# An encoder trunk on one core: where six weight pieces are split a second time

## The chip, the cores and the metric

The kernel runs on one core of a Trainium2 chip. The metric is the device time of one execution in microseconds (us). The engines are PE (TensorE, matrix products), DVE (VectorE), ACT (ScalarE), POOL (GpSimd) and SP (SyncE, which only issues transfers here). SBUF is the memory on the core, PSUM the accumulator memory in banks of 512 float32 per partition, DRAM the memory outside. Each engine works through its own instructions in order and waits for the others by semaphores.

## The reference

A two-layer encoder over a sequence of 2048 tokens (x_prompt) and one of 512 (x_sample), width 1024, all in float32.

```python
h = rmsnorm(x, g);  z = h @ w_in                      # 1024 -> 1024 (q) + 256 (k) + 256 (v) + 1024 (gate)
o = banded_gqa_with_sink(q, k, v, rel_bias, sink)     # 16 heads of 64, 4 k/v heads, |i-j| <= 128
x = x + (o * silu(gate)) @ w_out                      # layer 0
h = rmsnorm(x, g);  f = fftn(h, positions and 256 channels of each group).real
x = x + (f * silu(h @ w_gate)) @ w_out                # layer 1
y = rmsnorm(x, gf)
```

Both sequences go through the same weights. What the change touches is layer 0's projection weight w_in, 1024 x 2560.

## The kernel before

**Split products.** The products keep nearly float32 accuracy by splitting each operand in two parts of the type fp32r: a high part, which is a cast of the value, and a low part, which is the value less the high part. `matmul3` (lines 91 to 95) adds three products: high by high, high by low, low by high. So each weight piece must be split before use: one cast on ACT (line 107) and one subtract on DVE (line 114) or in four pieces on POOL (line 112).

**Weight pieces.** w_in is cut into 20 pieces of 128 x 1024 (512 KB): 0 to 7 are q for the eight head pairs, 8 and 9 are k, 10 and 11 are v, 12 to 19 the gate for the eight head pairs. Pieces 20 to 27 are w_out. A split piece has 1 MB (both parts) and lies in a tile `w`, of which there are four buffers (tag "w"). `load_w` (line 97) gives a piece to the caller.

**Chunks.** Layer 0 runs in five chunks of 512 tokens (`CHUNKS`): chunk 0 is the sequence of 512 tokens, chunks 1 to 4 are the long one. Chunk 0 loads the raw pieces from w_in and w_out, splits them and, for most, stores both parts in DRAM (`wsd`). Chunks 1 to 4 load the split parts from `wsd` in one transfer of 1 MB (line 101). The first six pieces that chunk 0 uses (8, 9, 10, 11, 0, 12; `LATE`, line 34) are needed at once at the start; they are split with DVE (`lo_engine`) and not stored then. Later in chunk 0, at one place in each of the head pairs 1 to 6 (lines 655 and 656), one of the six is loaded from w_in once more, into another `w` buffer, split with ACT and POOL, and stored to `wsd`. These are the tiles `w32late` and `wlate`; nothing in chunk 0 reads them.

**The order within a chunk.** `make_h` (line 166) loads x transposed in eight slices (`xk`), multiplies with the norm factor on POOL (line 180) and splits the slices into h, on ACT and DVE (lines 184 and 185); for a chunk that has a neighbour to its right there are 128 halo columns more (`hl`, lines 190 and 191). `kv_proj` (line 244) makes k (`kp`, two banks; 48 matmuls), the halo's k (`kh`), and v (`vp`, four tokens blocks in four banks, then one for the halo). k is copied to `kwin` by ACT and DVE in turn (lines 261 and 262), `kh` by ACT (line 283). Then the q and gate products of head pair 0 follow, and a loop over 64 steps (eight head pairs, four blocks of 128 tokens, two heads), with scores (line 396), exponential (line 412, ACT), transposes (line 432), their split (lines 433 and 434) and the product with v (line 446). Between these stand the q and gate products of the next head pair (`qp`, `gp`), and the tanh of the gate (line 351). During the last head pairs `stats` (line 135) makes the sums of squares for the next chunk (tiles `xs`), and `spread` (line 149) turns them into a row for the norm: DVE writes a diagonal `dg` (line 158), PE multiplies it with ones (`ib`, line 162).

**The seam between two chunks.** The output projection has two halves of four banks (`op`). The first half runs among the last steps of the loop. The second half, the `tail`, runs at the seam, followed by `kv_proj` of the next chunk. `evac` (line 508) adds the residual x to each of the four banks on DVE (line 516) in tiles `xr`, of which there are three buffers, and SP stores them to `x1d` (line 517). So the fourth residual tile of a half is loaded only when the first one of that half has been stored. There are six banks: k and v of the next chunk use those that the tail's evacuations free.

**Buffers that bear on the change.** The raw pieces, the slices `xk` and the tiles `xs` share four buffers of 4 KB per partition (`xtile`, tag "x"). Who comes later in the program waits until the one that had the buffer before is done. A scheduler places the instructions of each engine by its own estimate of their times within what data and buffers allow; lines 123 and 124 let the kernel add an order of issue.

Of the kernel before, what the change touches and what calls it, by code (L numbers as in the profile page):

```python
# [8 lines left out]
F32 = mybir.dt.float32  # L9
# [4 lines left out]
ALU = mybir.AluOpType  # L14
# [4 lines left out]
P = 128  # L19
D = 1024  # L20
# [10 lines left out]
BIG = 1.0e30  # L31
LINE = 512
HALVES = ((1, 0), (1, 1), (0, 0), (0, 1))
LATE = (0, 8, 9, 10, 11, 12)
CH = 512
CHUNKS = [(2048, SEQ, T), (0, 0, SEQ), (512, 0, SEQ), (1024, 0, SEQ), (1536, 0, SEQ)]

# [1 line left out]
def f32(ap):  # L39
    return ap.bitcast(F32)  # L40
# [3 lines left out]
def encoder(  # L44
# [3 lines left out]
    PE, ACT, DVE, POOL, SP = nc.tensor, nc.scalar, nc.vector, nc.gpsimd, nc.sync  # L48
# [22 lines left out]
    wsd = [dram.tile([P, 2, D], F32R, name=f"wsd{i}") for i in range(28)]  # L71
# [7 lines left out]
    def xtile(shape, dtype, name):  # L79
        return xp.tile(shape, dtype, align_bytes=LINE, tag="x", bufs=4, name=name)  # L80
# [13 lines left out]
        PE.matmul(out, a[0], b[1], start=False, stop=False, skip_group_check=more)  # L94
        PE.matmul(out, a[1], b[0], start=False, stop=stop, skip_group_check=more)  # L95

    def load_w(c, n, name, lo_engine=None, late=None):

        w = wp.tile([P, 2, D], F32R, align_bytes=LINE, tag="w", bufs=4, name=f"w{name}")
        if c:  # L100
            SP.dma_start(f32(w), f32(wsd[n]))
            return w[:, 0], w[:, 1]
        w32 = stage[late is not None or n > 19 or n in (6, 7, 18, 19)](f"w32{name}")
        load = SP.dma_start(w32, w_in[n] if n < 20 else w_out[(n - 20) // 4, (n - 20) % 4])
        if late:
            after(load, late)
        ACT.copy(w[:, 0], w32)  # L107
        if lo_engine is None:

            for i in range(4):  # L110
                cs = slice(i * 256, i * 256 + 256)
                POOL.tensor_tensor(w[:, 1, cs], w32[:, cs], f32(w[:, 0, cs]), ALU.subtract)
        else:
            lo_engine.tensor_tensor(w[:, 1], w32, f32(w[:, 0]), ALU.subtract)
        if late or n not in LATE:
            (SP if lo_engine else POOL).dma_start(f32(wsd[n]), f32(w))
        return w[:, 0], w[:, 1]

    stage, res_tile, ready = [], [], {}

    def after(ins, anchor):

        if anchor is not None:
            tc.add_manual_dep(ins.ins, anchor.ins.name, ISSUE, reason="issue order")

    def attention_phase():

        with ExitStack() as es:
# [6 lines left out]
            def stats(c):  # L135

                tok, lo_t, hi_t = CHUNKS[c]
                nt = min(640, hi_t - tok) // P
                ss = main.tile([P, 8], F32, tag="ss", bufs=2, name=f"ss{c}")

                def one(i):
                    xt = xtile([P, D], F32, f"xs{c}_{i}")
                    after(SP.dma_start(xt, x[tok + i * P : tok + (i + 1) * P, :]), last_exp[0])
                    sq = ACT.activation(xt, xt, AF.Square, accum_out=ss[:, i : i + 1])
                    after(sq, last_exp[0])

                return [lambda i=i: one(i) for i in range(nt)] + [lambda: inv_rms(ss, nt, f"inv{c}")]

            def spread(c, inv):

                tok, lo_t, hi_t = CHUNKS[c]
                nt = min(640, hi_t - tok) // P
                invb = ap.tile([P, 640], F32, tag="invb", name=f"invb{c}")
                for i0 in range(0, nt, 4):
                    m = min(4, nt - i0)
                    ps = bank(f"ib{c}_{i0}")
                    dg = ap.tile([P, 4, P], F32, tag="tmp", bufs=2, name=f"dg{c}_{i0}")
                    DVE.tensor_tensor(
                        dg[:, :m], ident.unsqueeze(1).to_broadcast([P, m, P]),
                        inv[:, i0 : i0 + m].unsqueeze(2).to_broadcast([P, m, P]), ALU.mult,  # L160
                    )
                    PE.matmul(ps[:, : m * P], ones, dg[:, :m].rearrange("p i q -> p (i q)"), start=True, stop=True)
                    ACT.copy(invb[:, i0 * P : (i0 + m) * P], ps[:, : m * P])
                return invb
# [36 lines left out]
            for i in range(WARM):  # L201
                PE.matmul(ps, idle[:, :P], idle, start=True, stop=True)

            early = [load_w(0, 8, "k0_0", DVE)]
            hs, halo = make_h(0, None)
            early.append(load_w(0, 9, "k0_1", DVE))

            def bias_rows():
# [27 lines left out]
            last_exp, last_evac, last_mul = [None], [None], [None]  # L236
# [7 lines left out]
            def kv_proj(c, hs, halo, norms=None, early=None):  # L244
# [9 lines left out]
                def evac_k(t, ps, n, wc):  # L254
                    ps = scaled(ps, invb, f"k{t}")
                    for j in range(2):
# [3 lines left out]
                        for rows in (slice(0, 64), slice(64, 128)):  # L260
                            ACT.copy(kw[rows, 0, cs], sp)
                            DVE.tensor_tensor(kw[rows, 1, cs], sp, f32(kw[rows, 0, cs]), ALU.subtract)

                wk = early or [load_w(c, 8 + t, f"k{c}_{t}", DVE) for t in range(2)]

                def wslice(w, k, c0, n):
# [341 lines left out]
            for c in range(len(CHUNKS)):  # L608

                if c > 1:  # L610
                    hs, halo = make_h(c, invb)
                for s in tail:
                    s()
                if c == 1:
                    hs, halo = make_h(c, invb)
                if c:
                    invb0 = kv_proj(c, hs, halo)
                else:
                    invb0 = kv_proj(c, hs, halo, first_norms, early)
                rowd, sk = bias  # L620
                uTs = []
                res = [{} for p in range(8)]
                at = [attention(c, p, res[p], uTs) for p in range(8)]
                for s in qg_proj(c, 0, hs, res[0], invb0):
                    s()
                at[0][0]()
                fill = []
                for i in range(64 + LAG + AVLAG):
                    p, n = divmod(i, 8)
                    if n == 0 and i < 64:  # L630
                        if p < 7:

                            fill = qg_proj(c, p + 1, hs, res[p + 1], invb0)
                            fill.pop(0)()
                            at[p + 1][0]()
                            if i == 0 and c == 0:

                                for s in fill[:8]:
                                    s()
                                fill = fill[8:]  # L640
                        else:
                            op = out_proj(c, uTs)
                            fill, rest, tail = op[:4], op[4:7], op[7:]
                    if c + 1 < len(CHUNKS):
                        if i == 24:
                            norm_steps = stats(c + 1)
                        if i >= 28 and i % 4 == 0 and norm_steps:
                            inv = norm_steps.pop(0)()
                        elif i == 56:
                            invb = spread(c + 1, inv)  # L650
                    if i in (4, 8, 12, 16) and c in EXTRA:
                        EXTRA[c].pop(0)()
                    if c == len(CHUNKS) - 1 and i in AHEAD:
                        AHEAD[i]()
                    if c == 0 and i % 8 == 3 and 1 <= p < 7:
                        load_w(0, LATE[p - 1], f"late{p}", late=last_exp[0])
                    if i < 64:
                        at[p][1](*HB[n])
                    k = i - LAG
                    if 0 <= k < 64:  # L660
                        at[k // 8][2](*HB[k % 8])
                    if i < 64:
                        m = len(fill) * (n + 1) // 8 - len(fill) * n // 8
                        todo = fill[len(fill) * n // 8 :][:m]
                        for s in todo[: m // 2]:
                            s()
                    k -= AVLAG
                    if 0 <= k < 64 and k % 2 == 1:
                        b = k % 8 // 2
                        at[k // 8][3](b)  # L670
                        if b % 2 == 1:
                            at[k // 8][4](b)
                    if i < 64:
                        for s in todo[m // 2 :]:
                            s()
                    elif rest:
                        rest.pop(0)()
            return tail

    def fourier_phase(tail):  # L680
        with ExitStack() as es:
# [522 lines left out]
            for i, f in enumerate(pend):  # L1204
                finish(*f, last=i == len(pend) - 1)

    fourier_phase(attention_phase())


# [96 lines left out]
```

## Time and profile before

| | us |
|---|---|
| three runs, median | 1679.39 |
| lowest and highest | 1677.16, 1682.95 |
| the profiled execution, time | 1680.38 |
| the profiled execution, span | 1678.6 |
| PE busy | 1648.0 (98% of the span) |
| DVE busy | 1182.3 (70%) |
| ACT busy | 874.6 (52%) |
| POOL busy | 392.1 (23%) |
| moved by DMA | 344.69 MB, 205 GB/s |

Times in the profile are counted from the span's start. Chunk 0 reaches to about 240 us, where the k products of chunk 1 begin. A line of a timeline has the start, the duration, the engine, the line of the kernel, the operation, the tile that is written and those that are read, and in brackets the idle time of the engine before it and what ended it. A line of the waits has the waiting engine and line, what it waited for, the sum, the count and the longest.

### The profile page before, as it was taken

Reading aid. Unit: us, or ns where it says so; the run is one execution under the profiler, and the core shown is the slowest. Engines: PE = TensorE matmul, PEld = TensorE weight load, DVE = VectorE, ACT = ScalarE, POOL = GpSimd, SP = SyncE. Lnnn points to the kernel's source line nnn. Section 1 sums busy time; section 2 is a strip of 40 time slices with the busy share of each in tenths; the row PEclk is TensorE's granted clock in tenths of the full one; section 3 lists DMA queues with packets and bytes.
Section 4 is the critical chain, followed back from the end, with each engine's and each line's share of the span. In section 5 each row is a group of like instructions: output and inputs, shape, how many; then the busy total and the mean of one; then the engine's idle time right before and its main releaser. Section 6 shows DMA issues by size and latency. Waiting matters only on the chain.

```text
span 1678.6 us, 25638 instructions
## 1 busy us (share of the span) xinstructions
PE 1648.0 (98%) x8980; PEld 1413.9 (84%) x8980; DVE 1182.3 (70%) x2782; ACT 874.6 (52%) x1998; POOL 392.1 (23%) x544
## 2 busy tenths in 40 slices
PE   9999899999999999999999999999999999999998
PEld 6887778888898888988888888888888887888886
DVE  5788645888638886478874588758676768888553
ACT  6788624676326674256752466646554455343321
POOL 2466740211403122221114211121112121111000
PEclk9999999999999999999999999999999999999999
DMA  8487775454765455763548644556556468453331
GB/s 306 154 330 308 262 285 207 167 197 161 261 226 186 174 185 180 272 223 132 183 151 318 250 151 164 212 199 221 190 205 236 171 229 338 158 194 126 122 126 51
DMA packets 91341, 344.69 MB, mean 205 GB/s; under 512 B 11163, under 2 KB 21403, under 8 KB 73292
## 3 DMA queue, kind: packets, MB, share of 16 engines
q1 hardware_dynamic: 73404, 267.79, 45.6%
q0 software_dynamic: 17520, 74.46, 11.3%
q8 instruction: 72, 1.18, 0.3%
q10 hardware_dynamic: 288, 0.79, 0.2%
q14 instruction: 57, 0.47, 0.1%
HBM read 267.47 MB, written 75.53 MB: 204 GB/s over the span
## 4 chain that ended last, share of the span: by engine, by line
PE 85%; DVE 5%; ACT 4%; DMA 3%; issue 2%; POOL 1%; SPq 0%; DVEq 0%; POOLq 0%; ACTq 0%
PE av L446 6%; PE spt L396 6%; PE pt L432 6%; PE qp L93 4%; PE qp L95 4%; PE qp L94 4%; PE gp L93 4%; PE gp L95 4%; PE gp L94 4%; PE op L93 4%; PE fo L94 4%; PE fo L95 3%; PE op L95 3%; PE op L94 3%; PE fo L93 3%; PE W L93 2%
## 5 line engine op out<-in xcount | busy, mean ns | idle before, releaser
L412 ACT ACTIVATE S<-S 128x385 f32<-128x385 f32 (+1 forms) x320 | 191.1, 597 | 40.5 <-DVE S L408 39.7
L433 ACT CAST pts<-pt 128x384 fp32r<-128x384 f32 (+1 forms) x320 | 144.6, 455 | 118.9 <-PE pt L432 114.5
L434 DVE TENSOR_TENSOR pts<-pt,pts 128x384 fp32r<-128x384 f32 (+1 forms) x320 | 168.6, 527 | 47.6 <-ACT pts L433 44.3
L408 DVE CUSTOM_DVE_ANT_0 S<-spt,b 128x385 f32<-128x385 f32 (+1 forms) x320 | 168.9, 528 | 37.0 <-PE spt L396 32.1
L396 PE MATMUL spt<-kwin,qab 128*128 128x384 f32 (+1 forms) x640 | 158.7, 329 | 1.6 <-DVE S L408 1.6
L461 POOL TENSOR_TENSOR o<-o,s 128x256 f32<-128x256 f32 x75 | 55.4, 738 | 429.5 <-DVE o L457 423.3
L432 PE MATMUL pt<-ident,S 128*128 128x128 f32 x896 | 150.5, 274 | 0.0
L396 PEld LDWEIGHTS spt<-kwin,qab 128*128 128x128 f32 x640 | 119.0, 188 | 29.4 <-DVE S L408 2.7
L446 PEld LDWEIGHTS av<-pts,v 128*128 128x128 f32 x896 | 126.7, 189 | 16.0 <-DVE pts L434 3.1
L446 PE MATMUL av<-pts,v 128*128 128x256 f32 x896 | 136.6, 285 | 2.9 <-DVE pts L434 2.0
L93 PE MATMUL qp<-h,wq 128*128 128x512 f32 x320 | 137.2, 429 | 0.7 <-ACT wq L107 0.7
L93 PE MATMUL gp<-h,wg 128*128 128x512 f32 x320 | 137.8, 431 | 0.0
L418 DVE TENSOR_SCALAR S<-S 128x384 f32<-128x384 f32 (+1 forms) x288 | 129.9, 451 | 8.5
L93 PE MATMUL op<-wo,uT 128*128 128x512 f32 x320 | 127.0, 398 | 2.9 <-ACT uT L463 2.9
L93 PE MATMUL fo<-wo,tTu 128*128 128x512 f32 x320 | 125.8, 393 | 1.3 <-ACT wo L1108 1.3
L432 PEld LDWEIGHTS pt<-ident,S 128*128 128x128 f32 x896 | 114.2, 140 | 14.7 <-DVE pts L434 3.4
L95 PE MATMUL qp<-h,wq 128*128 128x512 f32 x320 | 126.2, 394 | 0.1
L94 PE MATMUL op<-wo,uT 128*128 128x512 f32 x320 | 125.9, 394 | 0.0
L95 PE MATMUL gp<-h,wg 128*128 128x512 f32 x320 | 125.8, 393 | 0.0
L94 PE MATMUL qp<-h,wq 128*128 128x512 f32 x320 | 125.8, 393 | 0.0
L94 PE MATMUL gp<-h,wg 128*128 128x512 f32 x320 | 125.7, 393 | 0.0
L94 PE MATMUL fo<-wo,tTu 128*128 128x512 f32 x320 | 125.4, 392 | 0.1
(341 smaller groups left out, 4113.8 us busy)
## 6 DMA issues: line engine op xcount, KB each, us to landing
wq<-wsd SPq DMA_DIRECT2D x32, 1024.0 KB, 4.8
wg<-wsd SPq DMA_DIRECT2D x32, 1024.0 KB, 5.6
wo<-wsd SPq DMA_DIRECT2D x32, 1024.0 KB, 4.9
x<-x1d SPq DMA_DIRECT2D x40, 512.0 KB, 3.7
b<-b21d SPq DMA_DIRECT2D x40, 512.0 KB, 5.9
b<-rowd SPq DMA_DIRECT2D x40, 384.0 KB, 4.2
xs<-in_x_dram SPq DMA_DIRECT2D x23, 512.0 KB, 6.6
s2d<-gt POOLq DMA_DIRECT2D x40, 256.0 KB, 4.1
```

Source lines behind the costliest of these rows:

```text
L93: PE.matmul(out, a[0], b[0], start=start, stop=False, skip_group_check=more)
L94: PE.matmul(out, a[0], b[1], start=False, stop=False, skip_group_check=more)
L95: PE.matmul(out, a[1], b[0], start=False, stop=stop, skip_group_check=more)
L396: PE.matmul(ps[:, 2 + k0 * P : 2 + k1 * P], q, kwin[g][:, part, b * P + k0 * P : b * P + k1 * P], start=part == 0, stop=part == 1,)
L408: DVE.tensor_tensor_reduce(out=s[:, e0:e1], in0=ps[:, 1 + e0 : 1 + e1], in1=st["bias"][:, j, 386 - e1 : 386 - e0][:, ::-1], scale=1.0, sca ...
L412: last_exp[0] = ACT.activation(s[:, e0:e1], s[:, e0:e1], AF.Exp, bias=mn, scale=-1.0, accum_out=den)
L418: DVE.tensor_scalar(s[:, ks], s[:, ks], den, None, ALU.mult)
L432: PE.transpose(ps[:, kb, :], s[:, 1 + kb * P : 1 + (kb + 1) * P], ident)
L433: ACT.copy(hi[:, k0:k1, j, :], ps[:, k0:k1, :])
L434: DVE.tensor_tensor(lo[:, k0:k1, j, :], ps[:, k0:k1, :], f32(hi[:, k0:k1, j, :]), ALU.subtract)
L446: PE.matmul(out, v, pt[:, kb].rearrange("p h q -> p (h q)"), start=kb == k0 and part == 0, stop=kb == k1 - 1 and part == 1,)
L461: eng.tensor_tensor(of, of, res["s"][:, cs], ALU.mult)
```

## The change

The six pieces are no longer loaded and split a second time within chunk 0. Instead chunk 1 loads them raw where it needs them, splits them with ACT and DVE, uses them, and stores the parts to `wsd` from POOL's queue for chunks 2 to 4. The list keeps its members and has another name. The raw tiles take x buffers.

```diff
-LATE = (0, 8, 9, 10, 11, 12)
+AGAIN = (0, 8, 9, 10, 11, 12)
...
-    def load_w(c, n, name, lo_engine=None, late=None):
+    def load_w(c, n, name, lo_engine=None):
 
         w = wp.tile([P, 2, D], F32R, align_bytes=LINE, tag="w", bufs=4, name=f"w{name}")
+        if c == 1 and n in AGAIN:
+            w32 = xtile([P, D], F32, f"w32{name}")
+            SP.dma_start(w32, w_in[n])
+            ACT.copy(w[:, 0], w32)
+            DVE.tensor_tensor(w[:, 1], w32, f32(w[:, 0]), ALU.subtract)
+            POOL.dma_start(f32(wsd[n]), f32(w))
+            return w[:, 0], w[:, 1]
         if c:
             SP.dma_start(f32(w), f32(wsd[n]))
             return w[:, 0], w[:, 1]
-        w32 = stage[late is not None or n > 19 or n in (6, 7, 18, 19)](f"w32{name}")
-        load = SP.dma_start(w32, w_in[n] if n < 20 else w_out[(n - 20) // 4, (n - 20) % 4])
-        if late:
-            after(load, late)
+        w32 = stage[n > 19 or n in (6, 7, 18, 19)](f"w32{name}")
+        SP.dma_start(w32, w_in[n] if n < 20 else w_out[(n - 20) // 4, (n - 20) % 4])
         ACT.copy(w[:, 0], w32)
...
-        if late or n not in LATE:
+        if n not in AGAIN:
             (SP if lo_engine else POOL).dma_start(f32(wsd[n]), f32(w))
         return w[:, 0], w[:, 1]
...
-                    if c == 0 and i % 8 == 3 and 1 <= p < 7:
-                        load_w(0, LATE[p - 1], f"late{p}", late=last_exp[0])
```

In the order that the changed program has on each engine, the tail of chunk 0 and the start of chunk 1 stand as follows. SP: the last xk, the six raw loads in the order k, k, v, v, q, g, then the stores of the first three residual tiles, the load of the fourth and its store. DVE: the splits of h and hl, the two k subtracts, the first residual tile, a v subtract, two residual tiles, a v subtract, the fourth residual tile, four k parts of `kwin`, the q subtract, two k parts, the g subtract, two k parts. ACT: h and hl, four casts (k, k, v, v), four copies to `kwin`, the q cast, a copy to `kwin`, the copy `kh`, a copy to `kwin`, the g cast, two copies to `kwin`. POOL: the last xk product, then the six stores. PE's order is that of before but for four matmuls that have moved by a place or two.

## The prediction

> **What bounds the kernel now.** I read the page first, then PE's busy time in stretches, its waits, the chain of waits, and last the queues around the two places that the change touches.
>
> ```profile
> PE 1648.0 (98%) x8980; PEld 1413.9 (84%) x8980; DVE 1182.3 (70%) x2782; ACT 874.6 (52%) x1998; POOL 392.1 (23%) x544
> ...
> 120.00:140.00 20.00, 20.00 (x115) 17.39 (x114) 16.90 (x47) 18.60 (x45) 15.40 (x24) 1.00 0.81 315
> 160.00:170.00 10.00, 9.13 (x53) 7.71 (x52) 7.96 (x23) 6.59 (x17) 5.32 (x8) 1.00 0.82 329
> 170.00:180.00 10.00, 6.53 (x37) 4.92 (x35) 9.38 (x22) 8.72 (x20) 8.84 (x14) 1.00 0.64 217
> 180.00:190.00 10.00, 8.33 (x30) 6.55 (x31) 6.43 (x19) 5.76 (x16) 7.62 (x13) 0.66 0.97 366
> ...
> PE ib L162 <- DVE dg L158: 3.4, 1, 3.4
> PE op L93 <- ACT uT L463: 2.9, 1, 2.9
> PE spt L396 <- DVE S L408: 1.6, 1, 1.6
> ```
>
> Columns of the stretches: length, busy PE, PEld, DVE, ACT, POOL, granted clock, DMA share, GB/s. TensorE is the bound over the whole (98%), so only what opens or closes a gap on PE counts. The second half of chunk 0 is the exception: ACT is busy for 18.6 of 20 us, PE has gaps from 140 on, and the chain of waits runs over ACT, DVE and POOL there. There the removed work sits. The added work sits at the start of chunk 1, where PE has now almost no gap. So two stages are priced apart.
>
> **Part A, chunk 0: what goes away.** Six times: one SP load of 512 KB, one ACT cast, four POOL subtracts, one POOL issue and its 1 MB store.
>
> ```profile
> L112 POOL TENSOR_TENSOR wlate<-w32late,wlate x24: 725/740/867, 71.6 to 170.1; 128x256 fp32r<-128x256 f32 x24
> L107 ACT CAST wlate<-w32late x6: 1032/1037/1052, 70.5 to 166.9; 128x1024 fp32r<-128x1024 f32 x6
> ...
> 80.79 0.58 ACT L351 ACTIVATE th<-gp 128x512 f32<-128x512 f32 x1
> 98.59 0.60 ACT L351 ACTIVATE th<-gp 128x512 f32<-128x512 f32 x1
> 177.79 1.05 ACT L107 CAST wo<-w32o 128x1024 fp32r<-128x1024 f32 x1 [1.03 <-DMA wsd<-wlate]
> 178.74 0.59 ACT L351 ACTIVATE th<-gp 128x512 f32<-128x512 f32 x1
> ```
>
> The tanh of the gate comes once per head pair and marks the period. From 80.79 to 98.59 it is 17.80 us, with a late cast in it and PE full: there the late work is hidden, and the first two of the six are worth 0. The next four periods take 178.74 - 98.59 = 80.15, which is 80.15 - 4 x 17.80 = 8.95 more than PE needs. Each holds one late cast on ACT, the chain's engine: 4 x 1.04 = 4.15; in the last a cast also waits 1.03 for the late store to free its w buffer. A1 = 5.2, the floor for a chain through ACT without the wait being 4.2 and the ceiling 8.95 (PE full again). I take 5.2, the part with rows of its own. The 17.8 us of POOL subtracts (24 x 0.74) I price at nothing: POOL is not late, except as below; the first cover to fail would be uT, which queues on POOL behind them.
>
> Then the gap at 176 to 187.
>
> ```profile
> 180.00:182.00 2.00, 0.33 (x1) 0.36 (x2) 2.00 (x2) 1.37 (x2) 1.49 (x3) 0.62 1.01 422
> 182.00:184.00 2.00, 2.00 (x4) 0.97 (x4) 1.74 (x8) 0.24 (x1) 0.15 (x1) 0.50 1.03 354
> 184.00:186.00 2.00, 2.00 (x10) 1.98 (x9) 0.54 (x3) 1.15 (x4) 2.00 (x4) 0.50 1.01 410
> 186.00:188.00 2.00, 2.00 (x7) 1.55 (x6) 1.97 (x9) 2.00 (x8) 1.98 (x4) 0.67 0.87 322
> 216.00:218.00 2.00, 0.46 (x2) 0.02 (x1) 2.00 (x1) 0.59 (x2) 2.00 (x2) 1.00 1.02 433
> ...
> 177.15 0.41 DVE L408 CUSTOM_DVE_ANT_0 S<-spt,b 128x257 f32<-128x257 f32 x1
> 177.49 4.03 DVE L158 TENSOR_TENSOR dg<-ident,inv 128x512 f32<-128x512 f32 x1
> 177.51 3.46 POOL L112 TENSOR_TENSOR wo<-w32o,wo 128x256 fp32r<-128x256 f32 x5
> L158 DVE TENSOR_TENSOR dg<-ident,inv x8: 281/682/4034, 23.3 to 857.4; 128x512 f32<-128x512 f32 x5, 128x128 f32<-128x128 f32 x3
> ```
>
> PE stands still for 1.6 and 3.4 us, then runs at a clock of 0.50 to 0.67 until 188: the clock alone costs 2 x 0.5 + 2 x 0.5 + 2 x 0.33 = 2.7. The cause is dg, 4.03 against its median 0.68: beside it POOL runs five pieces of wo. Without the late pieces wo0_0_0 to wo0_0_4 move ahead in ACT's and POOL's order, so four pieces (4 x 0.74 = 2.96) are left beside dg, and dg stands one score operation (0.41) later. It loses then up to 2.96 - 0.41 = 2.55 instead of 4.03 - 0.68 = 3.35, or nothing if it starts first: 0.8 to 3.35 gained, I take the middle, 2.1. The gap left, 5.0 - 2.1 = 2.9, is like the 2.9 before 219, through which the clock stayed at 1.00, so I count the 2.7 as gained too. A2 = 4.8, ends 0 and 5.0 + 2.7 = 7.7. The gap before 219 is the last uT's own chain and stays. A = 10.0, from 4.2 to 16.7.
>
> [...]
>
> **Part B, the start of chunk 1: what is added.** Six loads of 512 KB take the place of six of 1 MB (6 MB less to read), and six ACT casts, six DVE subtracts and six POOL issues with 1 MB stores stand in the order of k, v, q, g. The loads wait for x buffers instead of w buffers.
>
> ```profile
> 241.07 0.39 ACT L190 ACTIVATE hl<-xk,g0s 128x128 fp32r<-128x128 f32 x1
> 238.89 1.67 DVE L191 SCALAR_TENSOR_TENSOR hl<-xk,g0s,hl 128x128 fp32r<-128x128 f32 x1
> 242.33 1.87 DVE L516 TENSOR_TENSOR xr<-xr,op 128x512 f32<-128x512 f32 x3
> 252.15 0.69 DVE L516 TENSOR_TENSOR xr<-xr,op 128x512 f32<-128x512 f32 x1 [7.95 <-DMA xr<-in_x_dram]
> L107 ACT CAST wv<-w32v x2: 1047/1052/1057, 13.4 to 21.8; 128x1024 fp32r<-128x1024 f32 x2
> L114 DVE TENSOR_TENSOR wk<-w32k,wk x2: 1226/1226/1226, 6.5 to 13.1; 128x1024 fp32r<-128x1024 f32 x2
> ...
> 243.03 2.43 SPq L517 DMA_DIRECT2D x1d<-xr  x3
> 246.12 0.34 SPq L492 DMA_DIRECT2D xr<-in_x_dram  x1
> xr<-in_x_dram SPq DMA_DIRECT2D x1, 256.0 KB, 5.9
> L541 SPq DMA_DIRECT2D w32g<-in_w_gate_dram x8: 384/414/461, 281.6 to 943.0; - x8
> DMA to landing us min/median/max: 5.5/6.2/7.0
> DMA to landing us min/median/max: 2.0/3.1/5.1
> DMA to landing us min/median/max: 2.0/5.9/9.9
> ...
> 241.25 0.39 PE L95 MATMUL kp<-h,wk 128*128 128x512 f32 x1
> 254.79 1.18 ACT L261 CAST kwin<-kp 64x512 fp32r<-64x512 f32 x2 [0.15 <-DVE kwin L262]
> 256.00 0.37 ACT L283 COPY kh<-kh 128x256 f32<-128x256 f32 x1
> 256.42 0.39 PE L93 MATMUL vp<-wv,h 128*128 128x256 f32 x1 [0.63 <-ACT kh L283]
> ```
>
> The three landing rows are those of the late loads, of the stores x1d<-xr in this stretch and of all xr. Step by step: (1) ACT is through with h and hl at 241.07 + 0.39 = 241.46; cast of wk1_0 to 242.5, subtract on DVE to 243.75. The third matmul of kp needs the low part: 243.75 instead of 241.25, +2.5. (2) w32k1_1 needs the x buffer of xk1_5, free at 238.89 + 1.67 = 240.56; with 5.5 to land (the least of the late loads; their median is 6.2), cast and subtract it is there at 248.4; PE asks at 243.75 + 22 x 0.227 (the spacing of the kp rows) = 248.7. Covered by 0.3. (3) On DVE the first xr evacuation of the tail stands behind both subtracts: 249.1 instead of 243.0. On SP its store stands behind w32q1_0 and w32g1_0, and w32g1_0 waits for the second subtract: store out at 249.2 instead of 243.03. (4) xr1_3 has three buffers to share, so its load waits for that store: 249.2 + 3.1 + 0.1 + 5.9, and 0.69 on DVE, is 259.0 instead of 252.84. (5) Behind it on DVE wait the k subtracts, for them ACT's k copies, and behind four of these the new wq cast and then the copy kh, whose bank the fourth v product needs. That was 256.37 - 252.84 = 3.53 after xr1_3; one k copy (0.59) less and a cast (1.05) more makes 4.0: 263.0. The fourth v product starts at 263.0 instead of 256.42: **+6.6**, the 2.5 of (1) within it. Ends: with fast transfers only (1) and the wq cast are left, +2.9; with a store of 5.1 and a load of 9.9 it is +12.7.
>
> (6) PE stands still for 1.2 us before the third v product (259.0) and 3.6 before the fourth, close to the 1.6 and 3.4 above: +2.7 of low clock, ends 0 and 2.7. **B = 9.3**, from 2.9 to 15.4. POOL's six stores are priced at nothing: behind them only the gate sums wait, whose data come at 281.6 and later. The stores to wsd land long before chunk 2 reads them. wq and wg have qp and some 13 us of v products as cover.
>
> [...]
>
> **Sum.** -10.0 + 9.3 = -0.7. The profiled execution took 1680.38 (span 1678.6), 1.0 above the median of 1679.39: 1679.7 against its own time, 1678.7 against the median. I give **1679.5**, no change. 0.3% is 5.0 us, about what this measurement can tell from no change.
>
> **Rivals.**
> Slower, the reload: xr1_3 comes at its long end, 9.9 instead of 5.9, because four 1 MB stores now run beside it. For it: its own row of 5.9 is among 1 MB loads too. Against: the stores are another queue. B = 12.7 + 2.7 = 15.4, net +5.4: 1685; it decides from a landing of some 9.5 us. Chance 0.18.
> Slower, the casts were not the bound: DVE and POOL set the period of 20.4, and ACT's idle 1.03 and 4.15 only shift. Then A is A2 alone, net 9.3 - 4.8 = +4.5 to +9.3 without A2 either: 1685 to 1689. For it: dg shows that POOL can hold up DVE. Against: ACT's 18.6 of 20. Chance 0.13.
> Faster, chunk 0 becomes PE-bound: A1 = 8.95, and dg starts first, A2 = 7.7: -16.7 + 9.3 = -7.4, 1672; with a quick boundary (2.9) less still. For it: the period of 17.80. Against: the q and g pieces still burden ACT. Chance 0.22.
> The clock rule: if (6) stays at 1.00, B = 6.6 and the time is 1677, within no change; chance 0.4 inside the forecast's.
>
> **Chances and range.** Forecast 0.47, the two slower rivals 0.31, faster 0.22. Range 1671 to 1688: 1672 and 1685 are inside, and about 0.1 is left on each side; the forecast's own range is 1674.5 to 1684.5.
>
> **What would show it.** Tanh periods of about 18 to 19 us between 98 and 180 (A1); dg's duration and the clock behind it (A2); kp's first wait near 2.5 us, the xr1_3 evacuation near +6 relative to kp, a PE wait of some 4 us at vp and the clock after it (B). Wrong makes it above all a w32 load that lands far from 5.5 us, or tanh periods that stay above 20.

## The result and the profile after

The changed kernel takes **1693.73 us** (median of 6 runs, 1689.3 to 1695.46) against 1679.38 before (6 runs beside them): a ratio of 1.0079, 95% interval 1.0062 to 1.0096. It is slower, by 14.35 us, and outside the range of the prediction. The profiled execution is one of its quicker ones, 1690.67 us with a span of 1688.9, so the trace shows 10.3 of the 14.35.

The page's busy times, then PE's stretches in chunk 0 and at the seam (columns as in the prediction), with one row of the kernel before at the end:

```profile
PE 1650.8 (98%) x8980; PEld 1416.2 (84%) x8980; DVE 1187.4 (70%) x2788; ACT 873.5 (52%) x1998; POOL 374.0 (22%) x520
...
60.00:80.00 20.00, 18.11 (x99) 15.40 (x98) 16.63 (x46) 14.30 (x36) 8.96 (x13) 0.95 0.45 178
80.00:100.00 20.00, 20.00 (x112) 17.47 (x111) 15.69 (x51) 15.81 (x40) 9.88 (x14) 0.96 0.42 159
180.00:190.00 10.00, 8.96 (x47) 6.65 (x46) 8.37 (x24) 8.40 (x22) 5.91 (x8) 1.00 0.93 339
240.00:250.00 10.00, 10.00 (x46) 8.29 (x45) 5.38 (x6) 3.15 (x3) 2.17 (x4) 1.00 0.99 365
250.00:260.00 10.00, 4.73 (x36) 4.33 (x34) 0.00 (x0) 1.16 (x2) 0.00 (x0) 0.95 0.88 361
260.00:270.00 10.00, 5.74 (x28) 5.45 (x29) 8.21 (x11) 5.74 (x9) 1.06 (x2) 0.54 0.38 158
...
60.00:80.00 20.00, 20.00 (x118) 17.51 (x117) 16.75 (x55) 17.20 (x43) 8.98 (x13) 1.00 0.44 155
```

POOL has lost 18 us of work and ACT 1, and the totals say nothing more. The stretches do. The gap before 190 is smaller and the clock behind it stays at 1.00. But from 60 to 80 there is a hole that the kernel before did not have (PE 20.00 there), and from 250 to 270 PE works for half the time, at a clock of 0.54 in the second ten. What PE waited for, from the two halves of the first 330 us:

```profile
PE av L451 <- DVE qab L350: 4.1, 3, 1.8
PE ib L167 <- DVE dg L163: 0.7, 2, 0.4
...
PE vp L93 <- DVE xr L521: 6.7, 1, 6.7
PE vp L93 <- ACT kh L288: 2.9, 1, 2.9
PE op L93 <- ACT uT L468: 2.9, 1, 2.9
```

The wait for dg fell from 3.4 to 0.7; the wait of av for qab rose from 0.8 to 4.1; at the seam stand 9.6 us of waits for the fourth residual tile and for kh, where before kh alone cost 0.6. The timelines of the seam (SP, POOL, VectorE and ACT), the landing times there (the median by tile, then shortest, median and longest of the four stores x1d<-xr) and SP's wait:

```profile
243.47 3.07 SPq L522 DMA_DIRECT2D x1d<-xr  x3
255.40 0.33 SPq L497 DMA_DIRECT2D xr<-in_x_dram  x1
240.28 0.58 POOL L105 DMA_DIRECT2D wsd<-wk  x1 [3.55 <-DVE wk L104]
247.62 0.53 POOL L105 DMA_DIRECT2D wsd<-wv  x1 [1.80 <-DVE wv L104]
260.66 0.69 DVE L521 TENSOR_TENSOR xr<-xr,op 128x512 f32<-128x512 f32 x1 [13.33 <-DMA xr<-in_x_dram]
250.50 1.26 ACT L266 CAST kwin<-kp 64x512 fp32r<-64x512 f32 x2 [5.25 <-PE kp L95]
286.32 0.59 ACT L347 ACTIVATE qab<-qp 64x512 fp32r<-64x512 f32 x1 [0.19 <-PE qp L95]
...
x1d<-xr SPq DMA_DIRECT2D x4, 256.0 KB, 12.8
xr<-in_x_dram SPq DMA_DIRECT2D x1, 256.0 KB, 5.2
DMA to landing us min/median/max: 2.0/12.8/13.8
SPq L497 <- DMA x1d<-xr: 8.8, 1, 8.8
```

Four stores of 1 MB go out on POOL's queue from 240.28 to 247.62. The residual's first store, issued beside them at 243.47, frees its buffer only 11.9 us later, when SP has waited 8.8 us for it; before it took 3.1. (The trace has no landing of this store itself; 12.8 is the median of those that it has, the last being the 2.0 of the store at 261. The recorded expectations call 12.8 the landing of the first store.) So the fourth residual tile's load is issued at 255.40 instead of 246.12 and its evacuation starts at 260.66 instead of 252.15. I take the time from the first copy of k to the first copy of q as the length of the seam: 286.32 - 250.50 = **35.8 us**. The same rows of the kernel before:

```profile
251.20 1.26 ACT L261 CAST kwin<-kp 64x512 fp32r<-64x512 f32 x2 [9.74 <-PE kp L95]
275.84 0.59 ACT L342 ACTIVATE qab<-qp 64x512 fp32r<-64x512 f32 x1 [0.26 <-PE qp L95]
```

That is 24.6. The seam grew by 11.2, and chunk 0 brought 0.7 (251.20 to 250.50): 10.5, which is the whole difference of the profiled executions. Of the 11.2, 9.0 are waits (9.6 less 0.6), and about 2.6 is the low clock (5.74 busy x 0.46).

### The profile page after: what moved, and what is told of

It reads as the page before. It is cut to its first block, busy times and chain, and to the rows that moved or that the text cites. A ratio compares the mean times of both kernels' runs of the same rounds, so it can differ in the third digit from the quotient of the medians.

```text
span 1688.9 us, 25604 instructions
## 1 busy us (share of the span) xinstructions
PE 1650.8 (98%) x8980; PEld 1416.2 (84%) x8980; DVE 1187.4 (70%) x2788; ACT 873.5 (52%) x1998; POOL 374.0 (22%) x520
## 3 DMA queue, kind: packets, MB, share of 16 engines
q0 software_dynamic: 17520, 74.46, 11.2%
## 4 chain that ended last, share of the span: by engine, by line
PE 75%; DVE 9%; DMA 6%; ACT 6%; issue 3%; POOL 1%; SPq 0%; DVEq 0%; POOLq 0%; ACTq 0%
PE av L451 4%; PE spt L401 4%; PE pt L437 4%; PE op L93 4%; PE op L95 4%; PE op L94 4%; PE fo L94 3%; PE fo L95 3%; PE fo L93 3%; PE qp L93 3%; PE qp L95 3%; PE qp L94 3%; PE gp L93 3%; PE gp L95 3%; PE gp L94 3%
```

## The experiments

**The two parts apart.** Four kernels were made for what the trace suggests: chunk 0 alone, the seam without either half of its supposed cause, and the six stores moved to the start of chunk 0.

*A place of its own for the fourth residual tile.* In the changed kernel:

```diff
+                    if c == 0 and (half, i) == (1, 3):
+                        place = ap.tile([P, 512], F32, tag="s", bufs=2, name="xr0_last")
                     if place is None:
```

> The changed kernel, with one edit: the fourth residual tile of chunk 0's second half lies in a buffer of the tag s, which is free by then, so its load waits for no store (in the changed kernel it is issued at 255.40, after a store that took 12.8 us to land, and its data end a wait of 13.33 us on VectorE). Theory (the slow store holds that load, and the load holds the third v product): the 6.7 us wait of PE for the xr evacuation goes, PE's clock behind it stays near 1.00, the first copy of qp comes at 278 to 280 instead of 286.32, and the time is 1684 to 1687 us, against 1693.7 of the changed kernel. Rival (the DMA engines are simply full from 240 to 260, 361 to 365 GB/s, and whatever loads there comes late): the tile still lands after 255, the time stays within 2 us of 1693.7. Rival (the wq cast and the kh copy behind the k evacuation hold the fourth product, whatever the tile does): the first wait goes and the second, 2.9, grows: 1690.

Measured: 1680.51 us, ratio to before 1.001 (0.9999 to 1.0021). Timeline of ACT and landing times:

```profile
252.54 2.59 ACT L266 CAST kwin<-kp 64x512 fp32r<-64x512 f32 x4 [3.80 <-PE kp L95]
276.61 0.59 ACT L347 ACTIVATE qab<-qp 64x512 fp32r<-64x512 f32 x1 [0.18 <-PE qp L95]
...
x1d<-xr SPq DMA_DIRECT2D x3, 256.0 KB, 11.9
```

The stores land as late as in the changed kernel (11.9), but nothing waits for them: the seam takes 24.1 us and the time falls by 13.2, more than the 7 to 10 expected. Neither rival holds; kh's wait is gone too. So of everything that the change adds to chunk 1, only the trip of that one tile through store and load is seen to cost time.

*No stores in chunk 1.*

```diff
-            POOL.dma_start(f32(wsd[n]), f32(w))
             return w[:, 0], w[:, 1]
         if c:
-            SP.dma_start(f32(w), f32(wsd[n]))
+            SP.dma_start(f32(w), f32(wsd[14 + n % 4 if n in AGAIN else n]))
```

> The changed kernel without the six stores of 1 MB on POOL's queue in chunk 1; chunks 2 to 4 read the parts of other pieces, of the same size, in their place, so the output is not the reference's. Loads, casts and subtracts of the six pieces in chunk 1 stay. Theory (the four stores issued from 240.28 to 247.62 fill the DMA engines and hold the residual's store, 12.8 us to land against 3.1 before): the first x1d store lands in 3 to 6 us, the load of the fourth residual tile is issued at about 248 to 250 instead of 255.40, the first copy of qp comes at 277 to 281 instead of 286.32, the time is 1684 to 1688. Rival (the store is late because it stands behind the six raw loads on SP's queue, 3 MB): the landing stays over 9 us and the time within 2 us of 1693.7.

Measured: 1682.44 us (0.9995 to 1.0022), below the 1684 to 1688 expected; the profiled execution took 1676.76. The median of the landings that the trace has of the residual stores is 2.3 us (12.8 in the changed kernel, 3.1 before), the fourth tile's load lands in 2.7 (5.2, 5.9 before), PE's wait for that tile (6.7) is gone and the one for kh is 0.8 (2.9, 0.6 before), and the seam takes 274.01 - 249.23 = 24.8. The six raw loads are still on SP's queue, so they are not what made the store late; the stores on POOL's queue are.

*Chunk 0 alone: the kernel before without the late splits.*

```diff
-            SP.dma_start(f32(w), f32(wsd[n]))
+            SP.dma_start(f32(w), f32(wsd[14 + n % 4 if n in LATE else n]))
...
-                    if c == 0 and i % 8 == 3 and 1 <= p < 7:
-                        load_w(0, LATE[p - 1], f"late{p}", late=last_exp[0])
```

> The kernel before with the six late splits of chunk 0 left out (their loads, casts, subtracts and stores); chunks 1 to 4 read the parts of other pieces, of the same size, in their place, so the output is not the reference's. This is the part of the change in chunk 0 alone. The forecast's reckoning (A1 5.2 and A2 4.8): 1669.4, tanh periods of 18 to 19 us. The reading of the changed kernel's trace (the period is not set by the late casts, only the gap before the spread closes; wo casts 2 to 3.7 us ahead at the seam): 1675.7 to 1677.4 and tanh periods near 20 from 98 to 180. Rival (nothing comes through chunk 0's end): 1679.4.

Measured: 1680.96 us, ratio 1.0007 (0.9996 to 1.0018). Not 1669.4, and not 1676 either: the part of the change in chunk 0 is worth nothing that can be told from zero. The waits of PE up to 210 us:

```profile
PE av L446 <- DVE qab L345: 4.9, 3, 1.9
PE av L446 <- DVE pts L434: 2.6, 1, 2.6
PE ib L162 <- DVE dg L158: 0.7, 2, 0.4
```

The gap at dg closes (3.4 to 0.7) and others open (0.8 to 4.9). Together the parts add up: 1.2 from this run and 13.2 from the place give 14.4, of 14.35 measured (medians of different rounds, in which the kernel before differs by 0.4).

*The stores at once, in chunk 0.* The six pieces are stored where they are first split, and not split again.

```diff
-        if c == 1 and n in AGAIN:
+        if 0:
...
-        if n not in AGAIN:
-            (SP if lo_engine else POOL).dma_start(f32(wsd[n]), f32(w))
+        (POOL if n in AGAIN else SP if lo_engine else POOL).dma_start(f32(wsd[n]), f32(w))
```

> The six pieces are split once, in chunk 0 as in both kernels, and their parts stored right there on POOL's queue; no late splits, none in chunk 1, which loads the parts as the kernel before does. Theory: 6 MB of stores fall into the stretch from 5 to 20 us, where the DMA engines of the kernel before are busy for 0.93 and more; at some 360 GB/s they are 17 us of transfers, of which perhaps half delays what PE waits for, so +8 at the start and the 2 to 4 us of chunk 0 gained: 1684. Rival (the stores find room in the stretch from 20 to 60, where the share falls to 0.25): 1676.

Measured: 1687.67 us (1.004 to 1.0077), later than both had it. The first tanh comes at 53.14 instead of 46.48, and what the start loses is not won back.

**Is it the store or the load that is late?**

*The stores held back on POOL until the third residual tile is done.*

```diff
+                        if (c, half, i) == (0, 1, 2):
+                            t = ap.tile([P, 8], F32, tag="vsc", bufs=2, name="third")
+                            third[0] = POOL.tensor_copy(t, xt[:, :8])
... (in load_w)
-            POOL.dma_start(f32(wsd[n]), f32(w))
+            after(POOL.dma_start(f32(wsd[n]), f32(w)), third[0])
```

> The changed kernel with its six stores on POOL's queue held back in POOL's order behind a small copy that reads the third residual tile, so that the first of them is issued at about 245 (with the first residual store out at 243.5) instead of 240.28; all of them still run, beside the load of the fourth tile. It parts the two steps in which that tile can be late: the store that frees its buffer (12.8 us to land in the changed kernel, 3.1 before) and its own load (5.2, 5.9 before). Theory (the store is what the four stores hold up): it lands in 3 to 7 us, the load is issued at 247 to 251, and the stretch from the first k copy to the first q copy (35.8, 24.6 before) takes 26 to 31; time 1682 to 1688. Rival (the load is then held up in the store's place, 10 us and more beside 4 MB of stores): stretch 33 to 36, time 1690 to 1694.

Measured: 1688.88 us (1.0027 to 1.0069), between the two ranges. Timelines of SP and POOL, and the landing times:

```profile
246.15 2.85 SPq L522 DMA_DIRECT2D x1d<-xr  x3
251.48 0.33 SPq L497 DMA_DIRECT2D xr<-in_x_dram  x1
249.79 1.11 POOL L105 DMA_DIRECT2D wsd<-wk  x2
...
x1d<-xr SPq DMA_DIRECT2D x4, 256.0 KB, 3.5
xr<-in_x_dram SPq DMA_DIRECT2D x1, 256.0 KB, 8.7
```

Now the first store frees its buffer within 5.3 us (246.15 to 251.48; the median of the landings is 3.5), and the load takes 8.7 instead of 5.2. The seam takes 286.32 - 252.73 = 33.6 us, in the rival's range. My theory that the store alone is the victim falls: beside the 4 MB it was the store that was late in the changed kernel (11.9 us, the load 5.2), and here it is the load (8.7, the store 5.3).

*The stores on SP's queue.*

```diff
-            POOL.dma_start(f32(wsd[n]), f32(w))
+            SP.dma_start(f32(wsd[n]), f32(w))
```

> The changed kernel with the six stores of chunk 1 on SP's queue instead of POOL's; in SP's order the store of wk1_0 then stands ahead of the three residual stores, that of wk1_1 ahead of the load of the fourth residual tile, and the raw loads of q and g behind them. Theory (the bytes do it, whatever the queue): the residual's store lands in 5 to 9 us, its tile's load comes at 250 to 254, the stretch from the first k copy to the first q copy (24.6 us before, 35.8 in the changed kernel) takes 28 to 33, the time is 1684 to 1690. Rival (it is POOL's queue that pushes SP's transfers aside): the stretch takes 24 to 26 and the time is 1680 to 1682.

Measured: 1684.7 us (1.0018 to 1.0052), in the theory's range. Landing times at the seam and SP's timeline:

```profile
wsd<-wk SPq DMA_DIRECT2D x2, 1024.0 KB, 5.9
x1d<-xr SPq DMA_DIRECT2D x4, 256.0 KB, 2.4
...
249.02 3.70 SPq L522 DMA_DIRECT2D x1d<-xr  x3
253.34 0.38 SPq L497 DMA_DIRECT2D xr<-in_x_dram  x1
```

The seam takes 283.21 - 255.50 = 27.7, just under the theory's 28 to 33. The first residual store frees its buffer within 4.3 us (249.02 to 253.34), less than the theory's 5 to 9; SP's own order lets out only one of the 1 MB stores ahead of it, and the raw loads of q and g now stand behind it. So this run does not part the queue from the bytes: before the fourth tile's load two of the 1 MB stores went out (at 245.40 and 252.81), four in the changed kernel. What it shows is that sending the same stores out in SP's order is worth 9.0 us of the 13.2.

*The place in the kernel before.* The same three lines as in the first run.

> The kernel before with the fourth residual tile in its own place and nothing else changed. Theory: PE waits there for 0.6 us only, so the place alone is worth nothing: 1679 to 1681. Rival (the tile's late load also costs through the k evacuation): the first q copy 1 us or more earlier relative to the first k copy, 1678.

Measured: 1678.77 us (0.9986 to 1.0012). Worth nothing there, as expected: before the change the trip fits.

**Why did chunk 0 not get shorter?** In the changed kernel, timelines of POOL, VectorE and PE:

```profile
69.57 2.83 POOL L117 TENSOR_TENSOR wq<-w32q,wq 128x256 fp32r<-128x256 f32 x4 [2.81 <-PE qp L95]
73.30 2.80 POOL L117 TENSOR_TENSOR wg<-w32g,wg 128x256 fp32r<-128x256 f32 x4
73.33 2.99 DVE L423 TENSOR_SCALAR S<-S 128x384 f32<-128x384 f32 x1
76.35 0.69 DVE L350 SCALAR_TENSOR_TENSOR qab<-qp,qab 64x512 fp32r<-64x512 f32 x1
77.09 1.08 PE L451 MATMUL av<-pts,v 128*128 128x256 f32 x4 [1.82 <-DVE qab L350]
```

And in the kernel before:

```profile
71.64 2.95 POOL L112 TENSOR_TENSOR wlate<-w32late,wlate 128x256 fp32r<-128x256 f32 x4 [4.37 <-ACT wlate L107]
80.84 2.82 POOL L112 TENSOR_TENSOR wg<-w32g,wg 128x256 fp32r<-128x256 f32 x4
73.34 0.65 DVE L418 TENSOR_SCALAR S<-S 128x384 f32<-128x384 f32 x1
```

The scaling of S takes 0.42 at its median (25 of them from 60 to 182). Here it starts 0.03 after POOL began four subtracts of wg and takes 2.99, until all four are done; qab stands behind it, and PE's av behind qab. In the kernel before the wg pieces ran 7.5 us later, behind those of wlate and wq, and the same scaling took 0.65, although it starts in the middle of the four wlate subtracts. So a run of subtracts does not hold VectorE to its end each time. Collisions were there before as well: the same 25 scalings had a median of 0.64, with the longest, 2.4 us, beside the wg pieces of later pairs. What the removal changed is which operations meet.

*No q and g subtracts on POOL in chunk 0*, on top of the run with the own place:

```diff
-        if lo_engine is None:
+        if lo_engine is None and n < 20:
+            POOL.dma_start(f32(w[:, 1]), w32)
+        elif lo_engine is None:
```

> The kernel of the run with the own place, and in chunk 0 the low parts of the q and g pieces of head pairs 1 to 7 are not computed on POOL: a transfer on POOL's queue copies the raw piece there instead, so the output is not the reference's. ACT's casts stay where they are; POOL loses 56 subtracts of 0.74 us. Theory (VectorE's in-place scaling of S, 0.42 us at the median, lasts 2.99, 2.43, 1.47 and 2.35 where it meets a run of these subtracts, and so sets the tanh periods of 18 to 21 us): all scalings of S stay under 0.6, the wait of av for qab (4.1 in all) goes, the tanh periods from 61 to 160 come to 17.8 to 18.5, the first k copy 5 to 8 us earlier than 252.54, the time 1673 to 1676, against 1680.5. Rival (ACT's chain of casts, exponentials and copies sets the period, as the forecast's A1 has it): periods as they are, 1680 to 1681.

Measured: 1676.05 us (0.9964 to 0.9992). Scalings of S from 60 to 182, and the second and the sixth tanh:

```profile
L425 DVE TENSOR_SCALAR S<-S x26: 338/388/3207, 59.9 to 181.1; 128x256 f32<-128x256 f32 x14, 128x384 f32<-128x384 f32 x12
61.38 0.60 ACT L358 ACTIVATE th<-gp 128x512 f32<-128x512 f32 x1
133.98 0.61 ACT L358 ACTIVATE th<-gp 128x512 f32<-128x512 f32 x1
```

Up to 134 the theory holds: no scaling over 0.6 until 163, and four periods take 72.6 us against 78.1 in the run with the own place (61.64 to 139.74) and 74.5 before. The wait of av for qab is gone. Behind that two other causes take most of it back: a 4.4 us wait of ACT for a tile xs, and the one scaling of 3.21, at 163, behind the casts of two wo pieces (158.03 and 159.37), whose subtracts were left on POOL. The first k copy comes at 248.97, 3.6 earlier, not 5 to 8, and the time is at the upper edge of what was expected. The run with the own place took 4.5 us more, and the two intervals do not touch.

*The q and g casts held back to where the kernel before has them*, on top of the own place (`exps` lists the exponentials so far, `PINNED` the pieces):

```diff
-        ACT.copy(w[:, 0], w32)
+        cast = ACT.copy(w[:, 0], w32)
+        if lo_engine is None and n in PINNED:
+            after(cast, exps[-4 if n < 8 else -3])
```

> The kernel of the run with the own place, and in chunk 0 the casts of the q and g pieces of pairs 3 to 7 are held back in ACT's order to where the kernel before has them: behind the exponentials of the pair before (75.14 and 77.96 in the kernel before, 68.74 and 70.30 without the late splits). No operation is added or left out. Theory (the removal moved these pieces, and with them POOL's subtracts, onto other VectorE operations): the 2.99 us scaling at 73 goes back to 0.65 and the 1.8 us wait of av with it, the third tanh comes within 0.5 of 80.8, and since the late subtracts are gone as well, the tanh at 178 to 181 comes 2 to 5 us earlier; time 1676 to 1679 against 1680.5. Rival (the place doesn't matter, some collision always comes): 1680 to 1682.

Measured: 1677.87 us (0.9988 to 1.0008). The collision at 73 is gone (no scaling over 0.6 until 115), and PE's 1.8 us wait with it; the third tanh comes at 81.39. But the tanh at 181.24 comes at 180.75 only, not 2 to 5 earlier. The time is where it was expected, and its interval overlaps that of the run with the own place, so its gain of 2.6 is not shown. ACT waits longer for xs: 5.0 us in three waits from 60 to 185, 3.1 in the run with the own place, 0.2 in the kernel before.

*Those waits taken away:* the square of a tile xs stands one step (four scores) later than its load, on top of the run above.

```diff
...
+                def step(i):
+                    if i < nt:
+                        one(i)
+                    if i:
+                        square(i - 1)
...
-                return [lambda i=i: one(i) for i in range(nt)] + [lambda: inv_rms(ss, nt, f"inv{c}")]
+                return [lambda i=i: step(i) for i in range(nt + 1)] + [lambda: inv_rms(ss, nt, f"inv{c}")]
```

> The kernel of the run with the casts as before, and the squares of the next chunk's statistics stand one step (four scores) later in ACT's order than their loads, in all chunks; no operation is added or left out. Theory (beside POOL's pieces, the loads of xs hold ACT and all behind it in the second half of chunk 0: 5.0 us in three waits in that run): the waits of ACT for xs go, the tanh at 180.75 comes 1 to 4 us earlier, 1674 to 1677. Rival (the waits lie beside others that end no earlier): 1677 to 1679.

Measured: **1674.04 us**, ratio to before 0.9975 (0.9963 to 0.9986). ACT's waits for xs are gone, and from the second tanh to the eighth it takes 115.7 us (63.64 to 179.36) instead of 118.6 (in a profiled execution of 1676.81). This version of the change, with the own place, the casts held back and the squares later, is faster than both kernels, than the kernel before by 0.25%.

*The later squares in the kernel before.*

> The kernel before with the squares of the statistics one step later and nothing else. It tells whether a gain of the run above belongs to the squares or needs the late work gone. Theory: ACT waits for xs for 0.2 us only in the kernel before, so 1679 to 1681. Rival (the later square loosens the collisions too): 1675 to 1678.

Measured: 1677.69 us (0.9984 to 1.0003). The median lies in the rival's range, but a gain is not shown. The run above is 3.6 us faster than this one, and five of its seven times lie below all ten of this one, so most of its gain needs the rest of the change.

## Why the prediction was wrong

Predicted was -10.0 + 9.3 = -0.7. Measured is +1.2 for A (chunk 0 alone) and 13.2 for B (undone by the place). Both sums failed, A by far the more (11.2 us, B by 3.9).

**A1 failed.** "5.2, the part with rows of its own", from the casts on ACT. The rows:

```profile
61.77 0.60 ACT L356 ACTIVATE th<-gp 128x512 f32<-128x512 f32 x1
101.59 0.60 ACT L356 ACTIVATE th<-gp 128x512 f32<-128x512 f32 x1
181.32 0.59 ACT L356 ACTIVATE th<-gp 128x512 f32<-128x512 f32 x1
...
62.28 0.60 ACT L351 ACTIVATE th<-gp 128x512 f32<-128x512 f32 x1
```

The four late periods took 79.73 instead of 80.15: 0.4 gained. The two before them, which the prediction set at 0 because PE was full there, took 39.8 (61.77 to 101.59) instead of 36.3 (62.28 to 98.59): 3.5 lost. So A1 was -3.1, not +5.2. The sentence that failed is "the 17.8 us of POOL subtracts I price at nothing". They were not a chain to be late in; they were runs of work beside which VectorE's operations last longer (0.42 became up to 2.99), and taking out one of three runs per pair moved the other two onto other operations, by 7 us in the pair shown. The prediction took operations out of a schedule as if the rest stayed in place. The floor of 4.2 "for a chain through ACT" was no floor. The rival "the casts were not the bound" had this right, with a chance of 0.13.

**A2 held, and was given back.** From the tanh at 178.74 to the next wo cast at 193.31 it took 14.57 us; now, 181.32 to 191.10, it takes 9.78: 4.8 gained, as forecast, with dg at 1.01 us and the clock at 1.00. That the sum fits so well is partly luck: dg gained 3.0 where 2.1 was taken. The 2.1 was the middle of a range whose upper end has dg lose nothing when it starts ahead of POOL's pieces, as the faster rival has it too; no run shows that: in the kernel before, dg started 0.02 us ahead of them (177.49, 177.51) and took 4.03. But the prediction counted on the next gap, 2.9 us before the output projection, leaving the clock alone as it had before. In the profiled execution of the changed kernel it did not (the last row is the kernel before):

```profile
216.00:218.00 2.00, 1.01 (x4) 0.77 (x5) 2.00 (x4) 1.47 (x4) 0.21 (x1) 1.00 0.27 99
218.00:220.00 2.00, 2.00 (x6) 1.52 (x6) 2.00 (x6) 1.57 (x3) 0.00 (x0) 0.50 0.61 170
220.00:222.00 2.00, 2.00 (x8) 1.57 (x7) 1.76 (x3) 0.23 (x1) 1.69 (x3) 0.65 0.86 306
...
218.00:220.00 2.00, 0.68 (x3) 0.49 (x4) 2.00 (x4) 1.14 (x3) 0.54 (x1) 1.00 0.41 151
```

2 x 0.50 + 2 x 0.35 = 1.7 lost, by a gap of the same length. From 60 to 100 there are 1.8 more (20 x 0.05 + 20 x 0.04), behind the new hole. So the clock's loss moved rather than went: -3.1, +4.8 and -1.7 leave nothing of A in this trace. This gap, PE's wait for uT, is 2.8 or 2.9 us long in twelve traces of this case. In stretches of 10 us around it the clock stays at 1.00 in three of them (the kernel before, that kernel with the place alone, and the casts held back without the later squares); in seven others, the changed kernel among them, the lowest stretch shows 0.80 to 0.90, and stretches of 2 us show 0.50 behind the gap in the changed kernel and in the run with the own place. What decides it is not shown. The prediction weighed both cases for B only, with its chance of 0.4 that (6) stays at 1.00.

**B: the path was right, two prices were wrong, and they partly cancelled.** What step (3) priced did not come: the first residual store went out at 243.47, 0.4 later than before, and not at 249.2. ACT was through with h and hl at 237.78 instead of 241.46, the second raw k piece was issued at 236.95 instead of 240.56, and its cast began 3.6 us later, where 5.5 was taken for the landing alone. Steps (4) and (5) are the path that was seen: the fourth tile's load waits for the first store, and k copies, the q cast and kh stand behind. The term that failed is the landing of that store in (4), 3.1 us, from the rows of before; the load went out 11.9 us after it. The load, priced at 5.9, took 5.2. Behind the failed term is "POOL's six stores are priced at nothing": they were looked at as instructions that someone might wait for, not as 4 MB beside a small transfer on PE's path. So (3) had 6.2 where 0.4 came and the store 3.1 where 11.9 came; that B as a whole, 9.3 forecast and 11.2 seen, is near is luck. The rival "reload" had the four stores and the place, but put the delay on the load; its argument against itself, "the stores are another queue", did not hold. The run with the stores held back shows that a delay of the load comes too (8.7), once the store escapes.

(1) did not show: PE did not wait for wk in the changed kernel's trace (the waits at the seam above have no kp), and 0.3 to 1.9 us in some of the other runs. (2) held. The q cast ahead of kh in (5) costs nothing by itself: with the place alone kh's wait is gone. (6) held: 2.6 of low clock against 2.7, behind waits of 6.7 and 2.9 us where 1.2 and 3.6 were taken. In the profiled execution B is 11.2 and in the medians 13.2; both lie within its ends of 2.9 to 15.4. The range as a whole missed because 4.2 was taken as the floor of A, and because each slower rival was priced with the other sum as forecast. Both came at once: the reload's 15.4 with nothing from A is 1679.4 + 15.4 = 1694.8, above the range's 1688.

## What to carry to other kernels

Before an operation is priced out of a tuned stage, look at what its neighbours on that engine will run beside once they move up; here the gain depended on where POOL's runs of subtracts fell on VectorE, and not only on how many there were (the scaling at 73 took 2.99 us beside those of wg and 0.65 beside those of wlate). A tile whose buffer is freed by a store and refilled by a load is a round trip through DMA: added traffic of some megabytes lengthened it here, by 11.2 us from POOL's queue and by 3.1 in SP's own order (the growth of the seam), and a buffer of its own (2 KB here) took the trip off the path (a seam of 24.1 us instead of 35.8). And each part of a change can be run alone: here the two runs added up to the whole difference, and showed that one of the parts had no gain to pay for the other.

## What the runs showed of the hardware

In the changed kernel a VectorE scaling that started 0.03 us after the first of four POOL subtracts (0.70 each) lasted until all four were done, 2.99 us in all; the median of the scalings is 0.42. POOL's subtracts lost nothing while VectorE's scaling lasted (2.80 for the four, 2.83 for the four wq pieces before them). It is not so each time: in the kernel before a scaling that starts within four such subtracts took 0.65. What decides between the two is not shown, and the start times do not tell it: in the kernel before dg starts 0.02 us ahead of POOL's five pieces by the rows and still lasts 4.03. The run without the q and g subtracts (no scaling over 0.6 until 163) shows that they were the cause.

Stores of 256 KB took 12.8 and 13.8 us beside four stores of 1 MB from another queue, with the DMA engines at a share of 0.99 and 365 GB/s, and the first of them no more than 11.9; without the 1 MB stores the median of the landings was 2.3. Whether it is the queue or the bytes is not shown; no run kept the bytes and changed only the queue.
